# Order of the loads between two stages of an expert layer: U's blocks by use, G's first part in another queue

## The chip, the cores and the metric

The kernel runs on one core of a Trainium2 chip. Five engines work side by side: PE (TensorE, matrix products; PEld is its weight load), DVE (VectorE), ACT (ScalarE), POOL (GpSimd) and SP (SyncE, which here only issues transfers). Transfers between DRAM and the core's memory are issued by SP, ACT or POOL, each in a queue of its own (q1, q10 and q0 in the profile), and are carried out by the core's 16 DMA engines, which all queues share. The metric is the device time of one execution in microseconds (us); lower is better.

## The reference

One encoder layer of 512 tokens with 1024 features: a combined projection, two kinds of attention, an output projection with LayerNorm, and then the part that matters here, a feed-forward layer of 16384 experts of which each token uses 128:

```python
idx = (e1 * PEER_N_KEYS + e2).reshape(PEER_CHUNK, PEER_HEADS * PEER_TOPK)
g = jax.nn.softmax(cv.astype(jnp.float32), axis=-1).reshape(PEER_CHUNK, -1).astype(xb.dtype)
u = u_table[idx]
hpre = jnp.einsum('td,ted->te', xb, u)
act = g * jax.nn.gelu(hpre, approximate=False)
return jnp.einsum('te,ted->td', act, v_table[idx])
...
h = layer_norm(DN_ALPHA * h + ffn + ple, ln2_g[i], ln2_b[i])
```

`u_table` and `v_table` have 16384 rows of 1024 numbers in fp32.

## The kernel before

The expert layer is done in two ways. For the first 128 tokens POOL fetches the 128 chosen rows of U and of V for each token out of DRAM by index (`gat`, one fetch of 128 x 1024 numbers, 512 KB, for one of the 128 choices), and DVE multiplies and adds them. For the other 384 tokens the layer is dense: the 16384 experts are 128 blocks of 128; for a block i PE multiplies the tokens with block i of U, ACT applies the GELU (line 1217, into a `ge` tile), the result is multiplied by the weights G, a dense matrix of tokens and experts that is nearly all zero, and PE multiplies that with block i of V into `acc`. fp32 operands of the V product and of the last U blocks are cut in two parts: ACT casts the upper part (`split`, line 110: `whi`, `v_hi`, `a_hi`), DVE subtracts to get the lower (line 111), and PE makes three products (`mm3`, lines 135 to 137).

The stage before the passage builds G and writes it to DRAM: `build_g` for one group of 128 tokens after another, stored from `g_st` by ACT's queue (line 1103) into `g_dram`. G has 24 parts of 16 tokens; parts 8 to 23 are written first, parts 0 to 7 last. In the same stage PE works off U's blocks 0 to 103 ahead, in plain fp32 (`lead_block`, line 1236, eight matmuls of 128 x 256 that the profile shows as 16 records). Each block is a load of 512 KB by SP's queue, into one of three buffers `raw`, and in the passage into the buffers `whi` (two) and `wlo` (two) of the same pool as well; DVE uses those until the last gathered rows of the stage (line 1143) are done. `psH` has two PSUM buffers `hp`, used in turn by the blocks of the passage; one is free again when ACT has taken its GELU.

The passage is the code from line 1506 on, written out by hand with the order of the engines as the code has it; only POOL's and ACT's places between other work are set by the scheduler that records it. There, the last loads of U are issued (`load_u`), G's first tile is loaded (`load_g(0, ...)`: 8 expert blocks wide, in two pieces, parts 8 to 23, 1 MB, and parts 0 to 7, 512 KB, into `g_near`), two V blocks are loaded (`load_v`, line 1447), and `blocks_ahead(n)` lets PE compute n of the last five blocks 99 to 103. One buffer of the row fetches is held back: a one-column copy by ACT from a `ge` tile into the buffer `gat` (line 1518) makes POOL's second fetch wait until that `ge` tile is there.

Behind the passage comes the main loop over 128 expert blocks: U's blocks 104 to 127 are computed in it (`expert_in`, loads at line 118, `hp<-hTh` in the profile), V is loaded, cut and multiplied (`expert_out`), `pair` multiplies G with the GELU (`g_near<-g_near,ge_ring`, line 1546) and cuts it (`a_hi`, `a_lo`), and POOL's fetches of rows run beside it. Further pieces of G are loaded in the loop by SP's queue in pieces of 512 KB.

Of the kernel before, what the change touches and what calls it, by code (L numbers as in the profile page):

```python
# [9 lines left out]
F32 = mybir.dt.float32  # L10
# [9 lines left out]
D = 1024  # L20
# [13 lines left out]
GT = 16  # L34
# [27 lines left out]
GATS = 8  # L62
# [17 lines left out]
def tile_encoder_layer(ctx: ExitStack, tc: tile.TileContext, A: dict, out: bass.AP):  # L80
    nc = tc.nc
# [114 lines left out]
    def ps_tile(name, bufs=2):  # L196
        return ps6.tile([128, 512], F32, name=name, bufs=bufs)
# [131 lines left out]
    with tc.tile_pool(name="ln0", bufs=1, reuse_waits="tile") as ln0, \  # L329
# [120 lines left out]
        for g in range(2):  # L450
            x = whole0[:, 4 * g:4 * g + 4]
# [367 lines left out]
    NTG = N_D // GT  # L819
# [10 lines left out]
    ge_t = {}  # L830
# [182 lines left out]
    for g in range(16):  # L1013
# [7 lines left out]
        raw = wst.tile([128, 8, 128], F32, name="raw", bufs=3)  # L1021
# [150 lines left out]
    gating = True  # L1172
    held_u = {}
# [7 lines left out]
    to_load = [i for i in lead_ids if i >= EARLY]  # L1181
# [18 lines left out]
    def load_u(name="raw"):  # L1200
        if to_load:
            i = to_load.pop(0)
            if not gating and name == "raw" and len(to_load) > 10:
                turn[0] += 1
                if turn[0] % 6 >= 3:
                    held_u[i] = (gate_place(turn[0] % 6 - 3, i), True)
                    return
            raw_t = wst.tile([128, 8, 128], F32, name=name, bufs=3 if name == "raw" else 2)
            ins = nc.sync.dma_start(raw_t, A["uT"][i])
            if i == first_load:  # L1210
                tc.keep_in_program_order(ins)
            held_u[i] = ([raw_t[:, k] for k in range(8)], name == "raw")

    def leave_u(i, ps):
        if i % 2 == 0:
            ge_t[i] = (ge_kept if SPILL <= i < KEPT else ge_free).pop(0)
        nc.scalar.activation(ge_t[i - i % 2][:, i % 2], ps[:, :N_U], AF.Gelu)
        if i < SPILL and i % 2:
            x = ge_t.pop(i - 1)
            nc.scalar.dma_start(ge_dram[i // 2], x.rearrange("p b t -> p (b t)"))  # L1220
            ge_free.append(x)
# [3 lines left out]
    def lead_block():  # L1225


        while sum(x[1] for x in held_u.values()) < (3 if gating or len(to_load) <= 10 else 6) and len(to_load) > 4:
            load_u()
        if not lead_ids:  # L1230
            return
        i = lead_ids.pop(0)
        raw = early_u[i] if i < EARLY else held_u.pop(i)[0]
        ps = psH.tile([128, 512], F32, name="hp") if gating else ps_tile("mm", 4)
        for k in range(8):
            nc.tensor.matmul(ps[:, :N_U], raw[k], whole[:, k, :], start=(k == 0), stop=(k == 7))  # L1236
            if k == 3 and last:
                leave_u(*last.pop())
            if k % 2 and tasks:
                tasks.pop(0)()  # L1240
            yield PRODUCT_U
        last.append((i, ps))
# [71 lines left out]
    def gate_and_leads():  # L1314
        nonlocal gating
        graw = [gate_raw(0), gate_raw(1)]
        for n in range(FIRST):
            if n == FIRST - 2:
                w, cut = gate_cut(graw.pop(0))
                tasks.extend([cut[0], nothing, cut[1]])  # L1320
            yield from lead_block()
        for j in range(16):
            if j % 8 == 0:
                while tasks:
                    tasks.pop(0)()
                gps = [ps_tile("mm", 4) for _ in range(4)]
            k = j % 8
            for c in range(4):
                cs = slice(c * 128, (c + 1) * 128)
                mm3(gps[c], (hTh[:, k, cs], hTl[:, k, cs]), w, k == 0, k == 7)  # L1330
                yield PRODUCT_G
            if j + 1 < 16:
                w, cut = gate_cut(graw.pop(0))
                if j + 2 < 16:
                    graw.append(gate_raw(j + 2))
                tasks[0:0] = [cut[0], nothing, cut[1]]
            if k == 7:
                gate_end(gps, slice(j // 8 * 512, j // 8 * 512 + 512), pls[-4:])
                yield from lead_block()
            for _ in range(STRIDE):  # L1340
                yield from lead_block()
            if 10 <= j < 14:
                pls.append(load_pl(j - 10, slice(512, 1024)))
# [82 lines left out]
    def load_g(tile_no, lo, hi, queue=nc.sync):  # L1426
        n, nb, views, j = g_all[tile_no]
        view = views[j]
        i = order[n]
        assert order[n:n + nb] == list(range(i, i + nb))  # L1430
        queue.dma_start(view[:, lo:hi].rearrange("p g b t -> p g (b t)"),
                        g_dram[lo:hi, :, i * GT:(i + nb) * GT].rearrange("g p x -> p g x"))
# [12 lines left out]
    def load_v(n):  # L1445
        raw = wst.tile([128, D], F32, name="raw", bufs=3) if in_wst(n) else pV.tile([128, D], F32, name="v_raw", bufs=3)
        nc.sync.dma_start(raw, v_rows[order[n] * 128:(order[n] + 1) * 128, :])
        return raw

    pG = ctx.enter_context(tc.tile_pool(name="pG", bufs=1, reuse_waits="tile"))  # L1450
# [4 lines left out]
    held_row = []  # L1455
# [37 lines left out]
    def cut_v(n):  # L1493
        vh = pP.tile([128, D], F32R, name="v_hi")
        vl = pP.tile([128, D], F32R, name="v_lo")
        split(vh, vl, v_next[n])
        return vh, vl

    def blocks_ahead(n):
        for _ in range(8 * n):  # L1500
            next(pe_work, None)
# [4 lines left out]
    with tc.manual_schedule(engines={nc.vector.engine, nc.scalar.engine, nc.tensor.engine, nc.sync.engine,  # L1506
                                     nc.gpsimd.engine}):
        gating = True
        for name in ("whi", "raw", "whi", "wlo"):
            load_u(name)  # L1510
        for lo, hi in ((128 // GT, NTG), (0, 128 // GT)):
            load_g(0, lo, hi, nc.gpsimd)
        v_next = [load_v(n) for n in range(2)]
        blocks_ahead(3)
        v_cut = {}
        v_cut[0] = cut_v(0)
        held_row.append(pG.tile([128, D], F32, name="gat", bufs=GATS))
        nc.scalar.copy(held_row[0][:, 0:1], ge_t[100][:, 0, 0:1])
        v_next.append(load_v(2))
        v_cut[1] = cut_v(1)  # L1520
        for _ in pe_work:
            pass
# [32 lines left out]
    with tc.manual_schedule(engines={nc.vector.engine, nc.sync.engine}):  # L1555
# [3 lines left out]
        for n, i in enumerate(order):  # L1559
            raw = v_next[n] if n < 3 else load_v(n)  # L1560
# [143 lines left out]
```

## Time and profile before

| | us |
|---|---|
| median of the timed runs | 1483.54 (three runs, 1483.13 to 1494.8) |
| the profiled execution | 1489.58 |
| its span, first to last instruction | 1487.8 |
| PE busy in it | 1444.5 (97%) |
| DVE busy | 1269.4 (85%) |
| POOL busy | 661.2 (44%) |
| ACT busy | 555.0 (37%) |

All times below are those of the profiled execution, counted from the start of its span. A row of the timeline names the start, the duration, the engine, the line of the code, the operation and `out<-in`, the tiles by their names in the code; in brackets stands the idle time of the engine before it and what ended that. `SPq` is SP's queue: the row is the issue, not the transfer. The DMA rows give packets, MB and the time that the packets took as a share of all 16 engines' time in the stretch.

### The profile page before, as it was taken

What the parts mean: (1) busy time and instruction counts of PE and PEld (TensorE: products, weight loads), DVE (VectorE), ACT (ScalarE), POOL (GpSimd) and SP (SyncE); (2) the same over time, 40 slices, a digit from 0 to 9 for tenths busy, and PEclk for the clock granted to TensorE, in tenths of its full rate; (3) what the DMA queues carried; (4) which work ended last, traced back from release to release, by engine and by line L of the source; (5) the groups of instructions that cost most, each with busy time, mean ns of one, the idle gap of its engine ahead of it and who ended that gap; (6) DMA issues with size and microseconds to landing.
All of it is one profiled execution on the core that took longest, in us unless ns stands there. A gap on an engine that the chain in (4) does not pass through costs nothing.

```text
span 1487.8 us, 21794 instructions
## 1 busy us (share of the span) xinstructions
PE 1444.5 (97%) x7667; PEld 1213.3 (82%) x7667; DVE 1269.4 (85%) x2638; ACT 555.0 (37%) x916; POOL 661.2 (44%) x533
## 2 busy tenths in 40 slices
PE   9999999999999999999999899999999999999996
PEld 5788777788888888888888788888788888878874
DVE  7476895668989999999999758897988989989998
ACT  5466784433211233123223233433333333323332
POOL 1013100053255543445335255686644757666660
PEclk9999999999999999999999999999999999999998
DMA  7342350293289999999989999999999999999992
GB/s 230 86 132 78 87 158 15 86 316 112 93 322 333 358 414 387 409 387 401 416 328 403 398 372 383 381 380 393 386 394 397 398 401 398 401 394 401 396 350 90
DMA packets 190653, 456.27 MB, mean 307 GB/s; under 512 B 16848, under 2 KB 80720, under 8 KB 187472
## 3 DMA queue, kind: packets, MB, share of 16 engines
q1 hardware_dynamic: 123504, 211.58, 39.6%
q0 software_dynamic: 58400, 208.69, 37.0%
q10 hardware_dynamic: 8640, 34.61, 5.7%
q8 instruction: 60, 0.98, 0.3%
q14 instruction: 49, 0.40, 0.1%
HBM read 412.62 MB, written 38.80 MB: 303 GB/s over the span
## 4 chain that ended last, share of the span: by engine, by line
PE 40%; DVE 25%; issue 14%; DMA 10%; POOL 5%; SPq 3%; ACT 2%; POOLq 0%; DVEq 0%; ACTq 0%
PE acc L136 5%; PE acc L135 5%; PE acc L137 5%; DMA v_raw<-in_v_rows_dram 4%; DVE base L1476 3%; PE pj L135 3%; PE pj L136 3%; PE pj L137 2%; SPq L1538 2%; DVE v_lo L111 2%; PE mm L135 2%; POOL row L1141 2%; POOL wlo L1141 2%; PE hp L1236 2%; PE hp L135 2%
## 5 line engine op out<-in xcount | busy, mean ns | idle before, releaser
L1474 POOL DMA_INDIRECT gat<-in_v_rows_dram,i_sel x128 | 218.3, 1705 | 117.0 <-DVE base L1476 96.5
L1459 POOL DMA_INDIRECT gat<-in_u_rows_dram,i_sel x97 | 157.8, 1626 | 92.7 <-DVE gat L1465 69.4
L136 PE MATMUL acc<-v_lo,a_hi 128*128 128x512 f32 x456 | 179.2, 393 | 4.0 <-DVE v_lo L111 4.0
L135 PE MATMUL acc<-v_hi,a_hi 128*128 128x512 f32 x456 | 177.8, 391 | 1.9 <-ACT v_hi L110 1.9
L137 PE MATMUL acc<-v_hi,a_lo 128*128 128x512 f32 x456 | 177.8, 390 | 0.0
L1476 DVE SCALAR_TENSOR_TENSOR base<-gat,hdot,base 128x1024 f32<-128x1024 f32 x128 | 164.1, 1282 | 1.8
L1236 PE MATMUL hp<-whole,raw 128*128 128x256 f32 x688 | 157.6, 384 | 4.8 <-DMA raw<-in_uT_dram 4.8
L111 DVE TENSOR_TENSOR wlo<-raw,whi 128x1024 fp32r<-128x1024 f32 (+3 forms) x103 | 117.9, 1147 | 50.9 <-ACT whi L110 45.2
L1236 PEld LDWEIGHTS hp<-whole,raw 128*128 128x128 f32 x688 | 130.8, 192 | 23.2 <-DMA raw<-in_uT_dram 4.7
L110 ACT CAST whi<-raw 128x1024 fp32r<-128x1024 f32 (+3 forms) x103 | 101.8, 989 | 122.2 <-DMA raw<-in_v_rows_dram 46.5
L110 ACT CAST v_hi<-v_raw 128x1024 fp32r<-128x1024 f32 x76 | 79.8, 1052 | 158.4 <-DMA v_raw<-in_v_rows_dram 110.8
L136 PE MATMUL acc<-wlo,a_hi 128*128 128x512 f32 x312 | 121.8, 390 | 2.4 <-DVE wlo L111 2.4
L137 PE MATMUL acc<-whi,a_lo 128*128 128x512 f32 x312 | 121.6, 390 | 0.0
L135 PE MATMUL acc<-whi,a_hi 128*128 128x512 f32 x312 | 121.0, 389 | 0.0
L1465 DVE SCALAR_TENSOR_TENSOR gat<-gat,h 128x1024 f32<-128x1024 f32 x97 | 114.5, 1223 | 0.0
L111 DVE TENSOR_TENSOR v_lo<-v_raw,v_hi 128x1024 fp32r<-128x1024 f32 x76 | 92.6, 1221 | 24.6 <-ACT v_hi L110 24.6
L136 PEld LDWEIGHTS acc<-v_lo,a_hi 128*128 128x128 f32 x456 | 85.7, 188 | 24.6 <-DVE v_lo L111 7.8
L135 PEld LDWEIGHTS acc<-v_hi,a_hi 128*128 128x128 f32 x456 | 85.7, 188 | 19.7 <-ACT v_hi L110 2.3
L137 PEld LDWEIGHTS acc<-v_hi,a_lo 128*128 128x128 f32 x456 | 85.7, 188 | 17.5
L1236 PE MATMUL mm<-whole,raw 128*128 128x256 f32 x400 | 93.0, 387 | 0.7 <-DMA raw<-in_uT_dram 0.7
L1236 PEld LDWEIGHTS mm<-whole,raw 128*128 128x128 f32 x400 | 75.9, 193 | 10.8 <-issue 1.0
L1141 POOL DMA_INDIRECT row<-in_u_rows_dram,s_ix x42 | 52.9, 1259 | 70.0 <-DVE row L1143 37.2
(425 smaller groups left out, 3476.4 us busy)
## 6 DMA issues: line engine op xcount, KB each, us to landing
raw<-in_uT_dram SPq DMA_DIRECT2D x92, 512.0 KB, 7.9
v_raw<-in_v_rows_dram SPq DMA_DIRECT2D x78, 512.0 KB, 12.1
raw<-in_v_rows_dram SPq DMA_DIRECT2D x50, 512.0 KB, 14.7
g_dram<-g_st ACTq DMA_DIRECT2D x24, 1024.0 KB, 9.2
ge_dram<-ge_ring ACTq DMA_DIRECT2D x36, 256.0 KB, 7.2
g_wide<-g_dram SPq DMA_DIRECT2D x9, 1024.0 KB, 18.2
raw<-in_w_q_dram SPq DMA_DIRECT2D x16, 512.0 KB, 4.2
g_near<-g_dram SPq DMA_DIRECT2D x15, 512.0 KB, 13.0
```

The source lines that it names most:

```text
L110: nc.scalar.copy(hi, src)
L111: nc.vector.tensor_tensor(lo, src, r32(hi), op=OP.subtract)
L135: nc.tensor.matmul(ps, a[0], b[0], start=start, stop=False)
L136: nc.tensor.matmul(ps, a[0], b[1], start=False, stop=False)
L137: nc.tensor.matmul(ps, a[1], b[0], start=False, stop=stop)
L1141: nc.gpsimd.indirect_dma_start(out=u[:np], out_offset=None, in_=u_rows, in_offset=bass.IndirectOffsetOnAxis(ap=ix[:np, k:k + 1], axis=0))
L1236: nc.tensor.matmul(ps[:, :N_U], raw[k], whole[:, k, :], start=(k == 0), stop=(k == 7))
L1459: nc.gpsimd.indirect_dma_start(out=u[:], out_offset=None, in_=u_rows, in_offset=bass.IndirectOffsetOnAxis(ap=i_sel[:, c, k:k + 1], axis=0))
L1465: nc.vector.scalar_tensor_tensor(u, u, 1.0, h[c], op0=OP.mult, op1=OP.mult, accum_out=hdot[:, c, k:k + 1])
L1474: nc.gpsimd.indirect_dma_start(out=u[:], out_offset=None, in_=v_rows, in_offset=bass.IndirectOffsetOnAxis(ap=i_sel[:, c, k:k + 1], axis=0))
L1476: nc.vector.scalar_tensor_tensor(base[c], u, hdot[:, c, k:k + 1], base[c], op0=OP.mult, op1=OP.add)
L1538: nc.sync.dma_start(ge.rearrange("p b t -> p (b t)"), ge_dram[order[n + GE_AHEAD] // 2])
```

## The change

Blocks 99 to 103 are all loaded by the passage's own list of buffers (the loop of `lead_block` before it stops one block earlier), in the order in which PE uses them. G's first piece (parts 8 to 23) moves from POOL's queue to SP's, behind those blocks and two V blocks; the second piece (parts 0 to 7) stays in POOL's. The copy that holds a row buffer reads the GELU of block 99 instead of that of block 100, and is written after two blocks instead of after three and V's first cut.

```diff
@@ -1225,7 +1225,7 @@
     def lead_block():
 
 
-        while sum(x[1] for x in held_u.values()) < (3 if gating or len(to_load) <= 10 else 6) and len(to_load) > 4:
+        while sum(x[1] for x in held_u.values()) < (3 if gating or len(to_load) <= 10 else 6) and len(to_load) > 5:
             load_u()
         if not lead_ids:
             return
@@ -1506,16 +1506,17 @@
     with tc.manual_schedule(engines={nc.vector.engine, nc.scalar.engine, nc.tensor.engine, nc.sync.engine,
                                      nc.gpsimd.engine}):
         gating = True
-        for name in ("whi", "raw", "whi", "wlo"):
+        for name in ("whi", "raw", "whi", "raw", "wlo"):
             load_u(name)
-        for lo, hi in ((128 // GT, NTG), (0, 128 // GT)):
-            load_g(0, lo, hi, nc.gpsimd)
+        load_g(0, 0, 128 // GT, nc.gpsimd)
         v_next = [load_v(n) for n in range(2)]
-        blocks_ahead(3)
+        load_g(0, 128 // GT, NTG)
+        blocks_ahead(2)
+        held_row.append(pG.tile([128, D], F32, name="gat", bufs=GATS))
+        nc.scalar.copy(held_row[0][:, 0:1], ge_t[98][:, 1, 0:1])
+        blocks_ahead(1)
         v_cut = {}
         v_cut[0] = cut_v(0)
-        held_row.append(pG.tile([128, D], F32, name="gat", bufs=GATS))
-        nc.scalar.copy(held_row[0][:, 0:1], ge_t[100][:, 0, 0:1])
         v_next.append(load_v(2))
         v_cut[1] = cut_v(1)
         for _ in pe_work:
```

In SP's queue the passage stood as follows before (`uT` is U, `raw_8208` block 99, `whi_8291` block 100, `raw_8293`, `whi_8295` and `wlo_8297` blocks 101 to 103, `raw_8375` and `raw_8407` blocks 104 and 105):

```order
L1209 DMA whi_8291<-in_uT_dram 128x1024
L1209 DMA raw_8208<-in_uT_dram 128x1024
L1209 DMA raw_8293<-in_uT_dram 128x1024
L1209 DMA whi_8295<-in_uT_dram 128x1024
L1209 DMA wlo_8297<-in_uT_dram 128x1024
L1447 DMA v_raw_8301<-in_v_rows_dram 128x1024
L1447 DMA v_raw_8303<-in_v_rows_dram 128x1024
L1447 DMA v_raw_8341<-in_v_rows_dram 128x1024
L118 DMA raw_8375<-in_uT_dram 128x1024
L118 DMA raw_8407<-in_uT_dram 128x1024
```

Now, with `whi_8289`, `raw_8291`, `whi_8293`, `raw_8295` and `wlo_8297` as blocks 99 to 103:

```order
L1209 DMA whi_8289<-in_uT_dram 128x1024
L1209 DMA raw_8291<-in_uT_dram 128x1024
L1209 DMA whi_8293<-in_uT_dram 128x1024
L1209 DMA raw_8295<-in_uT_dram 128x1024
L1209 DMA wlo_8297<-in_uT_dram 128x1024
L1447 DMA v_raw_8300<-in_v_rows_dram 128x1024
L1447 DMA v_raw_8302<-in_v_rows_dram 128x1024
L1431 DMA g_near_8271<-g_dram_3224 128x16x128
L1447 DMA v_raw_8341<-in_v_rows_dram 128x1024
L118 DMA raw_8375<-in_uT_dram 128x1024
L118 DMA raw_8407<-in_uT_dram 128x1024
```

Block 99's load has moved ahead of block 100's, and G's first piece stands between the second and the third V block, ahead of the loads of blocks 104 and 105.

On ACT the end of the passage stood as follows before (`hp_8308`, `hp_8318`, `hp_8328`, `hp_8350` and `hp_8360` are the products of blocks 99 to 103, `whi_8377` and `whi_8409` the casts of blocks 104 and 105, `gat_8339` the held row buffer):

```order
L1217 ACTIVATE ge_ring_3232<-hp_8308 128x256
L1217 ACTIVATE ge_ring_3232<-hp_8318 128x256
L110 CAST v_hi_8335<-v_raw_8301 128x1024
L1518 COPY gat_8339<-ge_ring_3232 128x1
L110 CAST v_hi_8343<-v_raw_8303 128x1024
L110 CAST whi_8377<-raw_8375 128x1024
L1217 ACTIVATE ge_ring_3232<-hp_8328 128x256
L1217 ACTIVATE ge_ring_3232<-hp_8350 128x256
L110 CAST whi_8409<-raw_8407 128x1024
L1217 ACTIVATE ge_ring_3232<-hp_8360 128x256
L1549 CAST a_hi_8439<-g_near_8273 128x768
```

Now (`hp_8330` is block 101, `gat_8325` the held buffer):

```order
L1217 ACTIVATE ge_ring_3232<-hp_8308 128x256
L1516 COPY gat_8325<-ge_ring_3232 128x1
L1217 ACTIVATE ge_ring_3232<-hp_8318 128x256
L110 CAST v_hi_8337<-v_raw_8300 128x1024
L110 CAST v_hi_8343<-v_raw_8302 128x1024
L1217 ACTIVATE ge_ring_3232<-hp_8330 128x256
L110 CAST whi_8377<-raw_8375 128x1024
L110 CAST whi_8409<-raw_8407 128x1024
L1217 ACTIVATE ge_ring_3232<-hp_8350 128x256
L1217 ACTIVATE ge_ring_3232<-hp_8360 128x256
L1550 CAST a_hi_8439<-g_near_8271 128x768
```

The copy has moved up by two places, the GELU of block 101 ahead of the cast of block 104, and the cast of block 105 ahead of the GELU of block 102 (`hp_8350`), whose PSUM buffer block 104 takes.

## Rows read from the trace of the kernel before

**Rows 1.** The page, engines: busy us (share) xinstructions.

```profile
PE 1444.5 (97%) x7667; PEld 1213.3 (82%) x7667; DVE 1269.4 (85%) x2638; ACT 555.0 (37%) x916; POOL 661.2 (44%) x533
```

**Rows 2.** Timeline of PE: start us, us, operation xcount [idle before].

```profile
845.22 3.24 PE L1236 MATMUL mm<-whole,raw 128*128 128x256 f32 x14
852.76 5.41 PE L1236 MATMUL hp<-whole,raw 128*128 128x256 f32 x16 [4.30 <-DMA raw<-in_uT_dram]
858.00 3.62 PE L1236 MATMUL hp<-whole,whi 128*128 128x256 f32 x16
861.46 3.62 PE L1236 MATMUL hp<-whole,raw 128*128 128x256 f32 x16
...
871.63 0.47 PE L135 MATMUL hp<-hTh,whi 128*128 128x256 f32 x1
```

**Rows 3.** Windows: PE, PEld, DVE, ACT, POOL busy, PEclk, DMA share, GB/s.

```profile
855.00:860.00 5.00, 5.00 (x20) 4.20 (x20) 0.00 (x0) 0.38 (x1) 1.91 (x2) 0.80 1.03 410
```

**Rows 4.** Timeline of SP's queue.

```profile
840.70 0.33 SPq L1209 DMA_DIRECT2D whi<-in_uT_dram  x1
841.13 3.29 SPq L1209 DMA_DIRECT2D raw<-in_uT_dram  x2
847.21 0.33 SPq L1209 DMA_DIRECT2D whi<-in_uT_dram  x1
...
848.13 1.56 SPq L1447 DMA_DIRECT2D v_raw<-in_v_rows_dram  x3
```

**Rows 5.** DMA issues of 840.70, 841.13, 848.13/848.67, 846.09: KB, us to landing.

```profile
whi<-in_uT_dram SPq DMA_DIRECT2D x1, 512.0 KB, 7.9
...
raw<-in_uT_dram SPq DMA_DIRECT2D x1, 512.0 KB, 11.6
...
v_raw<-in_v_rows_dram SPq DMA_DIRECT2D x2, 512.0 KB, 11.4
...
g_dram<-g_st ACTq DMA_DIRECT2D x1, 1024.0 KB, 8.9
```

**Rows 6.** DMA by queue, 844 to 849: packets, MB, engines' time.

```profile
q0 software_dynamic: 221, 0.88, 57.4%
```

**Rows 7.** DMA packets, 872 to 876.

```profile
DMA packets 461, 1.67 MB, mean 418 GB/s; under 512 B 53, under 2 KB 53, under 8 KB 461
```

**Rows 8.** DMA packets, 880.1 to 880.9.

```profile
DMA packets 474, 0.24 MB, mean 306 GB/s; under 512 B 3, under 2 KB 473, under 8 KB 474
```

**Rows 9.** DMA by queue, 889 to 893.

```profile
q0 software_dynamic: 330, 1.19, 77.2%
q1 hardware_dynamic: 501, 0.34, 26.7%
```

**Rows 10.** DMA issue of 881.70.

```profile
g_near<-g_dram SPq DMA_DIRECT2D x1, 512.0 KB, 17.1
```

**Rows 11.** Timeline of POOL.

```profile
857.69 0.90 POOL L1431 DMA_DIRECT2D g_near<-g_dram  x1 [16.64 <-DMA v_raw<-in_v_rows_dram]
...
863.34 1.75 POOL L1459 DMA_INDIRECT gat<-in_u_rows_dram,i_sel  x1 [3.43 <-ACT gat L1518]
...
872.62 1.50 POOL L1459 DMA_INDIRECT gat<-in_u_rows_dram,i_sel  x1 [0.30 <-issue]
```

**Rows 12.** DMA by queue, 857.7 to 860.9.

```profile
q1 hardware_dynamic: 355, 1.30, 102.3%
```

**Rows 13.** Timeline of ACT.

```profile
862.87 0.19 ACT L1518 COPY gat<-ge_ring 128x1 f32<-128x1 f32 x1
...
863.91 1.04 ACT L110 CAST whi<-raw 128x1024 fp32r<-128x1024 f32 x1
865.11 0.38 ACT L1217 ACTIVATE ge_ring<-hp 128x256 f32<-128x256 f32 x1 [0.16 <-PE hp L1236]
```

**Rows 14.** Waits of PE, 1000 to 1100, then 1280 to 1370.

```profile
PE acc L135 <- ACT v_hi L110: 1.9, 1, 1.9
...
PE acc L136 <- DVE v_lo L111: 2.1, 2, 1.5
```

## The prediction

> **What bounds the kernel now.** I read the page's engine lines first. The matrix engine (PE) is busy 1444.5 of 1487.8 us [rows 1], so what delays its stream in the passage delays the end, and only its idle or slow time there can be won. Next, PE's own timeline around the passage [rows 2]: the last run of fp32 matmuls of the stage before starts at 845.22 and lasts 3.24, so PE is free at 848.46; block 99 starts at 852.76, after 4.30 us of waiting for its load. It then takes 5.41 us where its successors take 3.62, and the mean granted clock between 855 and 860 is 0.80 [rows 3]: after the wait PE stood partly on the lower of its two levels (1.2 and 2.4 GHz). Blocks follow each other at 3.46 us (858.00 to 861.46), and the first split product of block 104 begins at 871.63. So the passage holds 4.30 + 1.79 = 6.1 us that an ideal change could win, 0.4% of the run. That is the whole stake on this side.
>
> Why the load was late: SP's queue issues a block into `whi` at 840.70 and block 99 behind it at 841.13 [rows 4]; they land 7.9 and 11.6 us later [rows 5], at 848.6 and 852.7. The order list shows that the one in front is block 100, which is needed second. Meanwhile G's first part moves in POOL's queue.
>
> **U's loads in the order of use: a gain of 6.0 us at block 99.** Block 99 now takes the place that landed at 848.6. With G's megabyte gone from POOL's queue (that queue had 57% of the transfer engines' time between 844 and 849 [rows 6]) it lands earlier rather than later; so the wait falls from 4.30 to between 0 and 0.2, and the slow 1.79 goes with it. Block 100 is issued at 841.13 and lands by 852.7 at the latest; it is needed at 848.5 + 3.5 = 852.0. G's 1.05 MB are 2.5 us of all transfer engines at 418 GB/s [rows 7], so I take 850. Block 101 still cannot be issued before 847.21, when the vector engine frees the second `whi` [rows 4]; blocks 102 and 103 follow at once. With 1.25 us for each 512 KB, the other half of the time going to the 1 MB store that the scalar engine issues at 846.09, they land at about 853, 854 and 855 and are needed at 855.4, 858.9 and 862.3. So the five blocks run without a gap and end at 848.5 + 5 x 3.46 = 865.8, 5.8 us before 871.63.
>
> **G's first part, behind two V blocks in SP's queue.** This term decides the sign. The two V blocks landed some 11.4 us after 848.13 and 848.67 [rows 5], at about 859.5 and 860; without the megabyte beside them I take 858 for both. Then G's megabyte starts, and behind it in the queue stand V's third block and the loads of blocks 104 and 105. In POOL's queue G went in packets of 4 KB (221 packets, 0.88 MB [rows 6]). In SP's queue the same kind of transfer goes in 512-byte packets: 474 packets, 0.24 MB, 306 GB/s with nothing beside them [rows 8]. Alone, 1.05 MB at 306 is 3.4 us. Against row fetches it is far dearer: between 889 and 893, when such a G load met them, the fetches moved 1.19 MB in 330 packets and SP's queue 0.34 MB in 501 [rows 9], and one G load of half the size took 17.1 us to land [rows 10].
>
> A rule of the Trainium skill speaks against the change here (DMA: Bandwidth & Descriptors, section Queues, rings and completion order): each transfer engine takes its queues in turn, one packet from each. The trace agrees [rows 9]. By that rule alone G would wait for every fetch there is, and the sum would be its late end below.
>
> **The rows, held until block 99.** Before, POOL issued G's second part at 857.69, after the store (846.09 + 8.9 = 855.0 [rows 5]), a first fetch behind it, waited until 863.34 for the scalar engine's copy, and issued the last of eight fetches at 872.62 [rows 11]. The copy came at 862.87 [rows 13] because it stood behind a V cast; now it stands behind the first GELU alone, near 852.5, and holds nothing: the second fetch follows the first. So nine transfers of 512 KB, 4.7 MB, 11.3 us at 418 GB/s, come from POOL's queue. None of its packets moved up to 860.9, 3.2 us after 857.69 [rows 12]; the store may land up to 3 us earlier now; so they begin between 858 and 861, and that is when G's first part is in SP's queue.
>
> **Blocks 104 and 105: the new wait.** From 858 the engines must move G (3.4 us), three loads of 512 KB (3.8 us) and up to 11.3 us of POOL's transfers. If these run from the start, G gets through only in their gaps and after them, and block 105 lands last: 858 + 3.4 + 3.8 + 11.3 = 876.5. If they start at 861, G is nearly through before them, the three loads share by halves, and 105 lands at 861.4 + 2 x 3.8 = 869. I take 874, nearer the late end, because rows 9 and 10 show what small packets get. PE needs block 104's `whi` cast; and in the scalar engine's new order the GELU that frees the PSUM buffer for block 104 stands behind the casts of both 104 and 105, where it stood ahead of the second before. So block 104 starts one cast and one GELU after block 105 lands, 1.04 + 0.38 [rows 13]: 875.4. PE then waits from 865.8 for almost 10 us, and I let the slow stretch move here: 1.8 us once more. Sum: 875.4 + 1.8 - 871.6 = **+5.6 us**, between +0.6 (869) and +8.1 (876.5). V's first casts and the product with G come within 5 us of block 105's landing, behind the 5.6 us of PE's blocks 104 and 105; if that cover were gone they would show as a wait of the first V product.
>
> **What becomes of it later.** The rows are fetched earlier than before, so the transfers that follow have a little more room. PE waited for late data again: 1.9 us for a V cast between 1000 and 1100, 2.1 us between 1280 and 1370 [rows 14]. I let these take back 1.6 of the 5.6, between nothing and 4.0: +4.0.
>
> The profiled execution took 1489.58 us (its span 1487.8); the median of the timed runs is 1483.54. The sum is a difference inside the span, so I add it to the median: **1487.5 us**.
>
> **Rivals.** (1) *G slips through: faster.* If POOL's first packets reach the engines after 861.5, G's small packets have them to themselves, and each further microsecond frees the loads behind it; with fetches from 865 on, block 105 lands at 861.4 + 3.8 = 865.2, block 104 starts at 866.6, 5.0 us early and without a slow stretch. Later waits for data would eat 1 us: 1479.5. For it: the store's landing is the starting gun and may stay at 855.0 or slip. Against: the copy no longer holds anything. (2) *No change.* The second half moves the same bytes, and PE waited there for data at least twice [rows 14]; gain or stall end in those waits, or the two terms cancel at a start near 871: 1483.5. (3) *The order does nothing.* Block 101 stays bound to 847.21; if it or block 100 is late, the wait only moves on by one or two blocks. But then PE still waits for blocks 104 and 105, so the time is that of my forecast. Speaking against it: the loads have 0.4 to 3 us in hand. (4) *Worse.* V's third block and G's next loads stay behind small packets for several blocks, as at 881.70 [rows 10]; a second stall of 8 to 10 us: 1497.
>
> **How the numbers follow.** Forecast 0.50, rival 1 0.22, rival 2 0.18, rival 3 0.03, rival 4 0.07. The range goes down to 1478.5, nearly all of rival 1's gain, and up to 1493.5: 1483.5 + 8.1 with the later waits taking nothing, and 2 for the difference between executions. About 1%, 14.8 us, is what a measurement of this kernel can tell from no change. The gain is capped at 6.1 us, the loss passes 14.8 only where rival 4 comes on top of the late end. So faster by over 1% 0.01, within 1% 0.96, slower by over 1% 0.03.
>
> **What would show it.** Block 99 starts within 0.3 us of 848.5 and the five blocks end near 865.8 (first term); G's first part takes over 12 us from issue to landing in SP's queue (second); the second fetch follows the first at once (third); block 104 starts after 870, with a wait for its cast or the GELU and a lower granted clock behind it (fourth). A start before 868 is rival 1. I would be wrong in the mechanism if G's packets in SP's queue were of 4 KB, or POOL's first packets came after 861.5.

## The result, and the profile after

The changed kernel is slower: 1500.98 us in the median of 17 runs (1492.38 to 1508.29), against 1493.21 us in 17 runs of the kernel before, a ratio of 1.0059 with a 95% interval of 1.0042 to 1.0075. That is 0.59%, 8.8 us of 1493.21 (the medians themselves lie 7.8 us apart), on the side that the forecast named and larger than it. The forecast also stood on a low base: the three runs shown first had a median of 1483.54, the 17 runs have one of 1493.21.

The profiled execution has a span of 1499.4 us (1487.8 before). Its engines line answers to [rows 1]; PE works as long as before, so all that was lost is idle time of PE:

```profile
PE 1444.8 (96%) x7667; PEld 1212.3 (81%) x7667; DVE 1271.7 (85%) x2638; ACT 555.3 (37%) x916; POOL 650.6 (43%) x532
```

PE's timeline in the passage, to be read beside [rows 2] (the last row is the first V product):

```profile
845.74 3.24 PE L1236 MATMUL mm<-whole,raw 128*128 128x256 f32 x14
848.81 3.62 PE L1236 MATMUL hp<-whole,whi 128*128 128x256 f32 x16
852.27 3.62 PE L1236 MATMUL hp<-whole,raw 128*128 128x256 f32 x16
...
862.63 3.62 PE L1236 MATMUL hp<-whole,wlo 128*128 128x256 f32 x16
880.20 0.58 PE L135 MATMUL hp<-hTh,whi 128*128 128x256 f32 x1 [13.96 <-ACT ge_ring L1217]
...
887.73 0.40 PE L135 MATMUL acc<-v_hi,a_hi 128*128 128x512 f32 x1
```

Block 99 starts without a wait and without a slow matmul, and block 103 ends at 866.2, 5.4 us before block 104 began in the kernel before. Then PE stands for 13.96 us. What it waits for is a GELU, but the scalar engine's timeline shows that the GELU was late because of the casts ahead of it, and these because of the loads of blocks 104 and 105:

```profile
852.88 0.19 ACT L1516 COPY gat<-ge_ring 128x1 f32<-128x1 f32 x1
...
860.93 1.04 ACT L110 CAST v_hi<-v_raw 128x1024 fp32r<-128x1024 f32 x1 [2.49 <-DMA v_raw<-in_v_rows_dram]
...
877.63 1.04 ACT L110 CAST whi<-raw 128x1024 fp32r<-128x1024 f32 x1 [15.36 <-DMA raw<-in_uT_dram]
878.82 1.04 ACT L110 CAST whi<-raw 128x1024 fp32r<-128x1024 f32 x1 [0.15 <-DMA raw<-in_uT_dram]
879.77 0.65 ACT L1217 ACTIVATE ge_ring<-hp 128x256 f32<-128x256 f32 x2
```

Block 105's load landed at 878.7, just ahead of its cast. In front of it in SP's queue stands G's first part, issued at 851.47; its completion is recorded at 874.99, 23.5 us later. The trace records sixteen landings for a load, as many as there are DMA engines, and the load is there with the last of them (block 104's fell at 877.53, and its cast began at 877.63); G's sixteen shares all came late, between 873.1 and 875.0. The queues between 860 and 870 (packets, MB, share of the engines' time) show it being starved, as in [rows 9]:

```profile
q0 software_dynamic: 944, 3.42, 88.2%
q1 hardware_dynamic: 940, 0.48, 16.4%
```

Packet for packet the two queues are level, but one of POOL's (q0) carries 3.6 KB on average and one of SP's (q1) 0.5 KB. This agrees with the rule that the prediction cited from the Trainium skill (DMA: Bandwidth & Descriptors, section Queues, rings and completion order): a transfer engine takes one packet from each queue in turn. Only when the fetches were nearly through had G the engines almost to itself, between 871 and 873:

```profile
q1 hardware_dynamic: 889, 0.54, 98.1%
q0 software_dynamic: 44, 0.11, 14.7%
```

POOL's timeline, against [rows 11], shows where the early packets come from: G's second part follows the last store, which landed at 851.4 (855.0 before), by 0.6 us, and no fetch waits for the copy.

```profile
852.03 0.96 POOL L1431 DMA_DIRECT2D g_near<-g_dram  x1 [17.10 <-DMA g_dram<-g_st]
853.29 1.00 POOL L1459 DMA_INDIRECT gat<-in_u_rows_dram,i_sel  x1 [0.31 <-issue]
854.59 0.95 POOL L1459 DMA_INDIRECT gat<-in_u_rows_dram,i_sel  x1 [0.30 <-issue]
```

The windows (columns as in [rows 3]) show PE at the lower level after the wait, until 884:

```profile
875.00:880.00 5.00, 0.00 (x0) 0.00 (x0) 1.30 (x2) 2.22 (x3) 0.00 (x0) 0.50 0.36 143
880.00:884.00 4.00, 3.80 (x18) 3.80 (x18) 2.68 (x3) 1.26 (x3) 0.00 (x0) 0.50 0.78 264
884.00:888.00 4.00, 4.00 (x34) 3.96 (x34) 1.23 (x1) 1.48 (x3) 0.00 (x0) 1.00 0.94 307
```

Between 875 and 880 the engines moved 143 GB/s: everything was waited for and little was left to move. Later nothing was given back: from the first V product to the end of the span the changed kernel took 611.7 us, the kernel before 610.2. PE's longest wait between 1000 and 1100, against [rows 14]:

```profile
PE acc L135 <- ACT v_hi L110: 2.1, 1, 2.1
```

### The profile page after: what moved, and what is told of

Its sections match the earlier page's. It is cut to its first block, busy times and chain, and to the rows that moved or that the text cites. A ratio compares the mean times of both kernels' runs of the same rounds, so it can differ in the third digit from the quotient of the medians.

```text
span 1499.4 us, 21790 instructions
## 1 busy us (share of the span) xinstructions
PE 1444.8 (96%) x7667; PEld 1212.3 (81%) x7667; DVE 1271.7 (85%) x2638; ACT 555.3 (37%) x916; POOL 650.6 (43%) x532
## 4 chain that ended last, share of the span: by engine, by line
PE 38%; DVE 22%; issue 15%; DMA 14%; POOL 5%; SPq 3%; ACT 2%; DVEq 0%; POOLq 0%; ACTq 0%
DMA raw<-in_v_rows_dram 5%; PE hp L1236 4%; DVE base L1476 4%; DMA v_raw<-in_v_rows_dram 4%; PE acc L136 3%; PE acc L137 3%; PE acc L135 3%; DVE v_lo L111 3%; PE pj L135 3%; PE pj L137 2%; PE pj L136 2%; DMA raw<-in_uT_dram 2%; PE mm L135 2%; PE mm L137 2%; PE mm L136 2%
## 5 line engine op out<-in xcount | busy, mean ns | idle before, releaser
L1474 POOL DMA_INDIRECT gat<-in_v_rows_dram,i_sel x128 | 210.6, 1645 | 125.8 <-DVE base L1476 105.5
```

Of the source, the lines that this page charges most:

```text
L1474: nc.gpsimd.indirect_dma_start(out=u[:], out_offset=None, in_=v_rows, in_offset=bass.IndirectOffsetOnAxis(ap=i_sel[:, c, k:k + 1], axis=0))
```

## The experiments

Each kernel is one edit of the kernel before or of the changed one, timed in five rounds beside runs of the kernel before (12 runs of each, but 10 with G in long packets and 6 with the rows as before). The table holds the ratio to before, and three lengths of the one profiled execution. "Passage" is the time from the end of the last `mm` run on PE (start plus duration) to the first V product; "G" and "105" are the landings of G's first part (when it is in SP's queue) and of block 105's load, counted from that same end. The end itself lay between 847.7 and 854.1 in these executions, with no order in it by edit, so the lengths are counted from there.

| kernel | ratio (95%) | passage | G | 105 |
|---|---|---|---|---|
| before | 1 | 29.1 | | 18.0 |
| changed | 1.0059 (1.0042, 1.0075) | 38.75 | 26.0 | 29.7 |
| U's order alone | 0.9978 (0.9964, 0.9993) | 26.8 | | 18.7 |
| early rows alone | 0.9990 (0.9973, 1.0007) | 25.4 | | 16.0 |
| G's move alone | 1.0047 (1.0022, 1.0072) | 37.9 | 23.1 | 29.5 |
| order + early rows, G in POOL's queue | 0.9997 (0.9984, 1.0011) | 24.5 | | 16.1 |
| order + G's move, rows as before | 1.0074 (1.0049, 1.0098) | 35.2 | 18.7 | 26.3 |
| changed, G in long packets | 1.0039 (1.0026, 1.0053) | 33.0 | 15.5 | 23.1 |
| changed, G in ACT's queue | 1.0014 (0.9996, 1.0033) | 31.7 | | 21.2 |
| changed, G behind 104 and 105 | 1.0043 (1.0026, 1.0060) | 31.6 | 30.0 | 19.0 |
| changed, rows held to block 102 | 1.0018 (0.9995, 1.0042) | 31.2 | 18.6 | 22.3 |
| order, rows held to block 102 | 1.0014 (0.9995, 1.0033) | 26.95 | | 17.1 |

The theories, as the expectations word them: A, G's 512-byte packets in SP's queue are starved by POOL's 4 KB packets, with the loads of blocks 104 and 105 behind them; B, the early fetches do the harm by themselves; C, G's place ahead of the loads and a stopped queue, whatever the packets; D, the small packets are slow whoever is beside them.

**G's first part back in POOL's queue** (the rest of the change stays):

```diff
-        load_g(0, 0, 128 // GT, nc.gpsimd)
+        for lo, hi in ((128 // GT, NTG), (0, 128 // GT)):
+            load_g(0, lo, hi, nc.gpsimd)
         v_next = [load_v(n) for n in range(2)]
-        load_g(0, 128 // GT, NTG)
```

> The change, with G's first piece back in POOL's queue ahead of the second; U's order and the early copy stay. Theory A (G's 512-byte packets in SP's queue are starved by POOL's 4 KB packets, and the loads of blocks 104 and 105 stand behind them): nothing small is left ahead of the loads; block 99 starts within 1 us of 848.5, block 104 between 866 and 870, no wait over 4 us, ratio to before 0.995 to 0.999. Theory B (the early fetches take the transfer engines, wherever G stands): block 104 starts at 876 or later, ratio 1.004 to 1.007. Theory C (G's place ahead of the loads and the stopped queue cost, whatever the packets and the fetches): as A.

PE's timeline in this kernel:

```profile
851.38 3.62 PE L1236 MATMUL hp<-whole,whi 128*128 128x256 f32 x16
...
866.72 3.72 PE L1236 MATMUL hp<-whole,wlo 128*128 128x256 f32 x16 [1.36 <-ACT ge_ring L1217]
...
876.02 0.40 PE L135 MATMUL acc<-v_hi,a_hi 128*128 128x512 f32 x1
```

Of the stall only 1.36 us are left, at block 103. So the loss needs G's move, and B falls. The ratio (0.9997) is just above what A expected (0.999 at most): the passage of this execution is 4.6 us shorter than before's, the timed runs show 0.4 us, with an interval that ends at 2.4.

**The rows held until block 100 again** (G stays in SP's queue):

```diff
-        blocks_ahead(2)
-        held_row.append(pG.tile([128, D], F32, name="gat", bufs=GATS))
-        nc.scalar.copy(held_row[0][:, 0:1], ge_t[98][:, 1, 0:1])
-        blocks_ahead(1)
+        blocks_ahead(3)
         v_cut = {}
         v_cut[0] = cut_v(0)
+        held_row.append(pG.tile([128, D], F32, name="gat", bufs=GATS))
+        nc.scalar.copy(held_row[0][:, 0:1], ge_t[100][:, 0, 0:1])
```

> The change, with the copy that holds the rows as it was before (GELU of block 100, behind V's first cast); G stays in SP's queue. Theory A: all fetches but the first come some 8 us later, so G is through by about 864 and block 104 starts at 867 to 871 with a wait of 2 to 5 us; ratio to before 0.998 to 1.001. Theory B: the same, since the fetches are later. Theory C: the wait for block 104 stays near 14 us, its start near 880, ratio 1.005 to 1.007.

A miss. Block 104 still waits 10.55 us. POOL's timeline says why the later copy is too little: the copy ends at 860.4, the second fetch goes out at once, and the six that follow it still share the engines with V's third block and blocks 104 and 105 one packet to one, so that these land 2.6 us apart instead of 1.25. Another part is G itself: fifteen of its sixteen shares had landed by 862.9, the last at 868.3.

```profile
858.43 0.99 POOL L1459 DMA_INDIRECT gat<-in_u_rows_dram,i_sel  x1 [0.30 <-issue]
860.61 1.72 POOL L1459 DMA_INDIRECT gat<-in_u_rows_dram,i_sel  x1 [1.19 <-ACT gat L1518]
```

**G's first part in long packets.** The same megabyte at the same place in SP's queue, read as contiguous runs of 8 KB:

```diff
-        load_g(0, 128 // GT, NTG)
+        nc.sync.dma_start(near[0][:, 128 // GT:NTG].rearrange("p g b t -> p (g b t)"), g_dram[128 // GT])
```

> The change, with G's first piece of the same megabyte in the same place of SP's queue, read as 8 KB of one row for each partition instead of sixteen runs of 512 bytes; the numbers loaded are other parts of G, so the output is not the reference's. Theory A: the packets are large, SP's queue gets half of the engines beside the fetches, G lands by 863 to 866, block 104 starts at 868 to 873 with a wait of 3 to 8 us; ratio to before 0.998 to 1.002. Theories B and C: nothing changes, block 104 near 880, ratio 1.005 to 1.007.

The DMA issue (KB, us to landing) and PE's timeline of this kernel:

```profile
g_near<-g_dram SPq DMA_DIRECT2D x1, 1024.0 KB, 12.9
```

```profile
873.51 0.58 PE L135 MATMUL hp<-hTh,whi 128*128 128x256 f32 x1 [7.34 <-ACT ge_ring L1217]
```

With long packets the two queues are level in bytes as well: between 860 and 870 SP's moved 2.16 MB in 509 packets and POOL's 1.91 MB in 516. In this execution that takes 10.6 us off G's transfer (23.5 to 12.9) and 5.75 off the passage. The timed runs show less: 3.0 of the 8.8 us, with intervals that overlap (1.0039 against 1.0059), where A expected 1.002 at most. So the small packets have a part in the loss, and the runs leave open how large it is. 3.9 us over before's passage remain with long packets too. That this rest is the price of G's place ahead of the loads while the fetches take every second packet, C's part, is argued and not shown.

**G's first part in ACT's queue**, ahead of the last store:

```diff
-        load_g(0, 128 // GT, NTG)
+        load_g(0, 128 // GT, NTG, nc.scalar)
```

> The change, with G's first piece in ACT's queue, where it stands ahead of the last store of G, at about 841 us. Theory A: the small packets go before the fetches come and hold up no load of U; block 99 starts by 850, block 104 between 866 and 870, the store lands 2 to 3 us later; ratio to before 0.995 to 0.999. Theory B: the fetches follow the store and still take the engines, block 104 at 873 or later, ratio 1.003 to 1.006. Theory C: as A.

```profile
852.01 3.72 PE L1236 MATMUL hp<-whole,whi 128*128 128x256 f32 x16 [0.67 <-DMA whi<-in_uT_dram]
...
871.46 6.00 PE L1236 MATMUL hp<-whole,wlo 128*128 128x256 f32 x16 [4.49 <-ACT ge_ring L1217]
```

A expected block 104 between 866 and 870 and a ratio of 0.999 at most; the block began at 877.1, a miss and where B had put it, while the ratio lies between the two. G landed at 855.8, and PE waits little for U. What is left is a wait of block 103 on the GELU of block 101, which stands on ACT behind the cast of block 104, whose load landed at 870.0. The ratio can't be told from 1.

**G's first part behind the loads of blocks 104 and 105**, in SP's queue:

```diff
         v_next = [load_v(n) for n in range(2)]
-        load_g(0, 128 // GT, NTG)
...
         for i in range(LEAD, LEAD + 2):
             expert_in(i)
+        load_g(0, 128 // GT, NTG)
```

> The change, with G's first piece in SP's queue behind the loads of blocks 104 and 105 instead of ahead of them. Theory A (small packets are starved by POOL's fetches): the two loads land before 870 and block 104 starts at 866 to 871, but G still needs 20 us or more and the first V product now waits for it; first V product 28 to 32 us after the stage before has ended on PE (before: 29.1, the change: 38.8), ratio to before 0.999 to 1.003. Theory C (only the place ahead of the loads costs): G follows in 4 us, the first V product comes after 23 to 26 us, ratio 0.995 to 0.998.

Its ratio misses what A and C expected, on the slow side; its lengths are those of A. The loads are no longer late, but G is: it took 22.4 us, and PE waits for it at the first V product, after an earlier wait of block 103.

```profile
g_near<-g_dram SPq DMA_DIRECT2D x1, 1024.0 KB, 22.4
```

```profile
866.78 5.41 PE L1236 MATMUL hp<-whole,wlo 128*128 128x256 f32 x16 [4.07 <-ACT ge_ring L1217]
...
880.52 0.50 PE L135 MATMUL acc<-v_hi,a_hi 128*128 128x512 f32 x1 [2.60 <-ACT a_hi L1549]
```

The passage is 2.5 us over before's, and the first V product runs partly at the lower clock (0.70 granted between 880 and 884): that of the next V block starts 9.2 us behind it instead of 7.0. So the starved transfer is the trouble, in whatever place it stands; C falls as the whole cause.

**One part of the change at a time**, on the kernel before. G's move alone:

```diff
-        for lo, hi in ((128 // GT, NTG), (0, 128 // GT)):
-            load_g(0, lo, hi, nc.gpsimd)
+        load_g(0, 0, 128 // GT, nc.gpsimd)
         v_next = [load_v(n) for n in range(2)]
+        load_g(0, 128 // GT, NTG)
```

> The kernel before, with G's first piece moved to SP's queue behind two V blocks and nothing else. Theory A: block 99 waits less, by 1 to 3 us, G meets the fetches and block 104 starts at 874 to 880; first V product after 33 to 37 us, ratio to before 1.002 to 1.006. Theory B (the early fetches alone cost): nothing is lost, block 104 at 867 to 871, ratio 0.997 to 1.000.

```profile
848.93 3.72 PE L1236 MATMUL hp<-whole,raw 128*128 128x256 f32 x16
...
878.54 0.58 PE L135 MATMUL hp<-hTh,whi 128*128 128x256 f32 x1 [12.08 <-ACT ge_ring L1217]
```

The loss is all there, but in this execution half of it comes about on one sixteenth of the loads. Fifteen shares of G had landed by 864.6, the last at 871.9; for block 105 the times are 872.2 and 878.3. G's issue, and the packets between 864 and 871:

```profile
g_near<-g_dram SPq DMA_DIRECT2D x1, 1024.0 KB, 22.3
```

```profile
DMA packets 815, 2.86 MB, mean 409 GB/s; under 512 B 80, under 2 KB 121, under 8 KB 815
```

Of the 512-byte packets 41 (121 - 80) passed in these 7 us, 5.9 per us, a sixteenth of the 94 per us of the changed kernel. That fits one engine out of sixteen that was behind with G when POOL's packets came and then served it packet for packet; why it was behind is not shown.

Block 99 starts without a wait here as well, with its load still behind block 100's: in this execution the 4.30 us of [rows 2] go when G's megabyte leaves POOL's queue, even in the old order.

U's order alone:

```diff
-        while sum(x[1] for x in held_u.values()) < (3 if gating or len(to_load) <= 10 else 6) and len(to_load) > 4:
+        while sum(x[1] for x in held_u.values()) < (3 if gating or len(to_load) <= 10 else 6) and len(to_load) > 5:
...
-        for name in ("whi", "raw", "whi", "wlo"):
+        for name in ("whi", "raw", "whi", "raw", "wlo"):
```

> U's order alone: five loads in the order of use, G's two pieces in POOL's queue and the copy that holds the rows as before. The first term of the prediction taken alone: block 99 starts without a wait, block 104 comes 22 to 25 us after the end of the stage before, ratio to before 0.995 to 0.998. Rival, that the gain ends in later waits: the same start, but a ratio of 0.999 to 1.001, as when G stood in POOL's queue with the early copy (0.9997).

```profile
851.54 3.72 PE L1236 MATMUL hp<-whole,whi 128*128 128x256 f32 x16 [1.08 <-DMA whi<-in_uT_dram]
855.75 3.72 PE L1236 MATMUL hp<-whole,raw 128*128 128x256 f32 x16 [0.50 <-DMA raw<-in_uT_dram]
...
867.97 3.72 PE L1236 MATMUL hp<-whole,wlo 128*128 128x256 f32 x16 [1.58 <-ACT ge_ring L1217]
```

Two short waits for loads in place of a long one, no slow matmul, and a new wait of 1.58 at block 103: the passage is 2.3 us shorter, the timed runs 3.3 us (1.0 to 5.4). Block 104 came 20.9 us after the end of the stage before, sooner than the 22 to 25 expected. This is the one version here whose interval lies below 1; the two others with this order and G in POOL's queue can't be told from 1.

The early rows alone:

```diff
-        blocks_ahead(3)
+        blocks_ahead(2)
+        held_row.append(pG.tile([128, D], F32, name="gat", bufs=GATS))
+        nc.scalar.copy(held_row[0][:, 0:1], ge_t[98][:, 1, 0:1])
+        blocks_ahead(1)
         v_cut = {}
         v_cut[0] = cut_v(0)
-        held_row.append(pG.tile([128, D], F32, name="gat", bufs=GATS))
-        nc.scalar.copy(held_row[0][:, 0:1], ge_t[100][:, 0, 0:1])
```

> The kernel before, with the copy that holds the rows reading block 99's GELU and written after two blocks, as in the change, and nothing else. Theory A: the second fetch comes 2 to 4 us earlier, block 99 waits as before, block 104 within 2 us of 871.6; ratio to before 0.999 to 1.002. Theory B: block 104 at 874 or later, ratio 1.003 to 1.006.

No difference that can be measured: fetches that begin earlier meet nothing but SP's 4 KB packets in the passage, and blocks 99 to 104 follow each other without a gap after block 99's wait. This run also shows how far a length of one execution can be trusted. Block 99's load stands where it stood before, yet the wait for it was 2.26 us instead of 4.30 and its matmuls took 3.72 instead of 5.41; these two, which the edit does not touch, make up the whole 3.7 us by which the passage is shorter. Differences of that size in the table say little by themselves.

**The fetches taken out of G's way.** The copy reads the GELU of block 102 and stands, on ACT, behind the casts of blocks 104 and 105, once with the change and once with U's order alone:

```diff
         for _ in pe_work:
             pass
+        held_row.append(pG.tile([128, D], F32, name="gat", bufs=GATS))
+        nc.scalar.copy(held_row[0][:, 0:1], ge_t[102][:, 0, 0:1])
```

> The changed kernel, but the copy that holds a row buffer reads the GELU of block 102 and stands on ACT behind the casts of blocks 104 and 105; so of POOL's transfers only G's second part and one fetch (1 MB) can meet G's first piece in SP's queue, and the other seven fetches cannot. Theory A (G's 512-byte packets are starved by POOL's 4 KB packets): G's first piece lands within 10 us of the V blocks, not later than 867 (after: 875), blocks 104 and 105 near 869 and 870, block 104 starts near 871 to 872, the passage is 29 to 31 us (before 29.1, after 38.75), ratio to before 0.998 to 1.003. Theory D (the small packets and the stopped queue are slow by themselves, whoever is beside them): G still lands after 871, block 104 starts after 876, passage over 34 us, ratio 1.004 to 1.008. Fetches that start some 14 us later than in the changed kernel may cost something later in the loop; e12 says how much.

> The same late copy (GELU of block 102, behind the casts of 104 and 105) with G's first piece in POOL's queue as before, so the order of U's loads and the late rows alone. Theory A: no small packets in SP's queue and hardly any fetch beside the loads, so blocks 104 and 105 land earlier than with the order alone and block 104 starts without a wait of over 2 us; passage 24 to 27 us; ratio to before 0.995 to 0.999 if the loop has room for rows that come later, 0.999 to 1.003 if it has not. Theory D says the same of this run.

In the first of them only G's second part and one fetch meet G's first part. The queues between 860 and 866:

```profile
q1 hardware_dynamic: 2038, 1.19, 70.7%
q0 software_dynamic: 180, 0.68, 38.8%
```

SP's packets pass at 340 per us instead of 94, block 105 lands 7.4 us sooner than in the changed kernel (22.3 against 29.7), and the passage is 31.2 us, 0.2 outside A's 29 to 31 and far from D's 34. G (870.2) and block 105 (874.0) landed 3 to 4 us past A's figures on the clock; 2.7 of that is the stage before, which ended later in this execution, and fifteen of G's sixteen shares had landed by 864.9, 3.6 us behind the same shares of V's second block; the last came at 870.2. D falls. The late rows have their own price further on: PE's wait between 1000 and 1100 grows from 1.9 to 7.1,

```profile
PE acc L135 <- ACT v_hi L110: 7.1, 1, 7.1
```

and in the second kernel to 3.2. From the first V product to the end of the span that kernel took 613.7 us against 610.2 before, which fits that its passage, 2.2 us shorter than before's, shows nothing in the timed runs.

## Why the prediction came out as it did

**U's loads in the order of use, 6.0 us: right in size, the cause not the order alone.** Block 99 starts at once, and the five blocks end at 866.2 (865.8 forecast). But the order alone takes away 3.2 of the 4.3 us and leaves new waits of 0.50 and 1.58; with the order and other rows, G still in POOL's queue, block 99 starts at once (both runs); G's move alone takes away all of the wait too; and the wait itself was 2.26 in the run with neither. So the 4.30 can't be shared out between the two. The prediction mentioned the lighter queue only as a help.

**G's first part in SP's queue: right.** 512-byte packets, level with POOL's packet for packet, 23.5 us to landing where over 12 was the sign. The rule is borne out by the changed kernel's 940 and 944 packets; [rows 9], from which the prediction read it, has 501 and 330, which are not level.

**The rows, held until block 99: right that nothing holds, wrong in the moment.** The prediction let the packets begin between 858 and 861. They began at about 856.3, because the store landed 3.6 us earlier than before and POOL followed it by 0.6 us instead of 2.7; that the two could add up was not allowed for.

**Blocks 104 and 105: the step that failed.** The prediction put block 105's landing between 869 and 876.5 and took 874; it was 878.7. All of G fell under the fetches, the late end, and the late end was itself too early by 2.2: it let both V blocks be there at 858, and the second, which POOL's packets already met, landed at 860.9. It also reckoned with the sixteen engines as with one: fifteen shares of block 105 were there at 877.8 and the last at 878.7. In G's move alone, where most of G was through early, that last share came 6 us behind the others (878.3 against 872.2). From the landing on the working holds: cast and GELU took 1.5 us (1.42), the slow stretch cost 1.6 (887.73 - 880.20 = 7.5 us from block 104 to the first V product, 5.9 before; 1.8 forecast). The passage grew by 9.6 us where +5.6 was forecast.

**What becomes of it later, -1.6: it was 0.** From the first V product on, the next 22 start 7.0 us apart in the kernel before and in the changed one alike: PE sets the pace there, and a later start moves all of it. The wait near 1050 is 2.1 instead of 1.9.

**The base: the other step that failed, and the larger in us.** The difference was added to 1483.54, a median of three runs. With a median of 1493.21 for the same kernel, 9.7 of the 13.5 us between forecast and measurement come from the base and 3.8 from the sizes above; counted from 1493.21, the stated range would have reached to 1503.2 and held the 1500.98. The profiled execution, 1489.58, had already stood 6 us higher than that median of three.

Of the rivals, "G slips through" asked for first packets after 861.5 and did not come; the run that gives G that room has a passage 2 us over before's, not 5 under it, since G's own transfer still stands ahead of the loads and its last share came at 870.2. "Worse" did not come either: there is one stall, not two.

What stays open: why the order with early rows, whose passage is the shortest of all (24.5 us), is not faster in the timed runs than the order alone. Each length is from one execution, and the end of the stage before differs by up to 6 us between executions. Open, too, is how the loss is shared between G's small packets and its place in SP's queue. What the runs show together is that it needs G in that queue while the fetches run: it goes with G back in POOL's queue, and most of it goes with the fetches taken away.

## What to carry to other kernels

Before a load is moved to another queue, look at the packets that the same transfer makes there, and at those of the queues that run beside it: where queues are served packet for packet, a transfer in 512-byte packets beside one in 4 KB packets got a seventh of the bytes here, and what stood behind it in its queue waited with it. Put such a load where nothing with large packets runs, or leave it in the queue that makes large packets of it; reading it in long runs took back 3.0 of 8.8 us here. Look at the last of a load's shares, not at the bulk of its packets: in one run here it landed 7 us behind the other fifteen. And a median of three runs is a poor base for a forecast of a few us where single runs of the same kernel lie 15 us apart.

## What the runs showed of the hardware

A queue behind a starved transfer can stop the engine that issues. In the changed kernel the issue of V's third block, next after G's first part, lasted 16.37 us, and the loads of blocks 104 and 105 could be issued only then:

```profile
851.47 0.38 SPq L1431 DMA_DIRECT2D g_near<-g_dram  x1
851.90 16.37 SPq L1447 DMA_DIRECT2D v_raw<-in_v_rows_dram  x1
868.38 13.10 SPq L118 DMA_DIRECT2D raw<-in_uT_dram  x5
```

With the same megabyte in long packets the issue took 0.43:

```profile
851.79 0.43 SPq L1447 DMA_DIRECT2D v_raw<-in_v_rows_dram  x1
```

With the rows held to block 102 it lasted 12.05 us and ended 5.8 us before G landed. What the stopped issue cost in the changed kernel is not shown, since no run frees it and leaves the rest; both loads landed right behind G there (at 877.5 and 878.7), 1.2 us apart.
